# Stores of split weights issued from GpSimd's queue instead of SP's, in a hybrid decoder step

## The chip, the cores and the metric

The kernel runs on one core of a Trainium2 chip. The time is the device time in microseconds. The kernel before took 2448.59 us in the median of three runs (2443.82 to 2450.43). A profile is one further execution, in which every engine's instructions and every transfer were recorded.

## The reference

One layer of a decoder, for a prompt of 4096 rows and 8 single sample rows, all in float32, D_MODEL = 1024:

```python
u, zp, q, k, v, za, gp, ga = split_projection(rmsnorm(xp, g_norm[l]), w_in[l])
pooled = multiscale_pool(u, 0, seq)                       # trailing means over 2/4/8/16 rows
att = attn_prompt(q, k, v, rel_bias, attn_sinks[l])       # window of 128, sinks, T5 bias
pg = einsum(pooled, w_grp)                                # per channel group
br_pool = (pg * pool_scale * silu(z_pool)) @ w_br_pool
br_attn = (att * silu(z_attn)) @ w_br_attn
merged = sigmoid(g_pool) * br_pool + sigmoid(g_attn) * br_attn
y = rmsnorm(x + merged @ w_out, g_final)
```

The large pieces are the input projection (1024 columns in, 4352 out, by groups of 128 columns), the two branch projections and the output projection.

## The kernel before, in words

The rows are worked through in eight chunks of T = 512 (chunk 1 carries the 8 sample rows too). A product is made with three matmuls in a reduced float32 format: every operand is split into a high half and a low half (what the high half leaves over), and high x high, high x low and low x high are added up (`mm3`, L175 to L177). A weight tile `w` is [128, 2, 4, 128]: the two halves of four 128x128 blocks, 512 KB. `split_into` makes it from a raw tile `wr`: ScalarE copies the high half (L136), VectorE or GpSimd subtracts to get the low half (L137). In chunk 0 VectorE always subtracts; from chunk 1 on GpSimd does it for some.

The input projection takes two column groups and two row halves as a 2x2 block product with seven multiplications in place of eight (`Pair`). Three of its seven weights (11, 12, 22) are raw quarters. The other four (s1 to s4) are sums and differences of quarters. In chunk 0 they are made by VectorE in `combined` (L196, tiles `sr` and, in place, `wr`), split, multiplied, and also written to a DRAM tile `s...`, so that later chunks load the finished halves and neither add nor split. The 16 weight tiles of the output projection (`so`) and that of the group maps (`swg`) are treated in the same way. This is `kept(key, make)`: the first time a key is seen the tile is split and stored (the store is L169), afterwards it is loaded (L165). There are 68 + 16 + 1 = 85 stores, all in chunk 0.

Buffers set the pace. `w` tiles come from a ring of five; when `more_weights` has run, near the end of chunk 0, three of every eight tiles come from a second ring of three. A buffer of the ring can be filled again when TensorE has read it and, in chunk 0, the store has read it too. Raw tiles come from two rings of four (`wr`, and `wr0` that exists in chunk 0 alone), and pairs of 512 columns of x and intermediate results from a ring of five (`H`).

At the end of a chunk the output projection runs (L165 or L169 for its weights, L847 for the residual), and between its column groups the next chunk's x is loaded (`prep_xt`, L364), normalised and split into the seven combinations `xt`. The reload of the first stored weight for chunk 1 is the seam between chunks 0 and 1.

All DMAs before the change are issued by SP, one queue, in order: an issue that waits for a semaphore holds all that come behind it. A scheduler that places instructions by the operations' assumed costs fixes, when the program is built, each engine's order of instructions; nothing is reordered on the chip. GpSimd's own work in chunk 0 is the power that makes the inverse root (L297), copies of the carry of the pooling (L673, L695), of the last block's keys and values (L626, L627) and of the sample rows' x (L366).

Of the kernel before, what the change touches and what calls it, by code (L numbers as in the profile page):

```python
# [10 lines left out]
F32 = mybir.dt.float32  # L11
# [35 lines left out]
def split_kernel(ctx, tc, i, o):  # L47
    nc = tc.nc
# [86 lines left out]
    def split_into(w, raw, eng=None):  # L135
        nc.scalar.copy(w[:, 0], raw)  # L136
        (eng or nc.vector).tensor_tensor(out=w[:, 1], in0=raw, in1=w[:, 0].bitcast(F32), op=ALU.subtract)  # L137

    def wtile():
        if "p1" in place:  # L140
            place["n"] += 1
            if place["n"] % 8 >= 5:
                cnt[0] += 1
                return place["p1"].tile([P, 2, 4, P], F32R, tag="w2", name=f"w_{cnt[0]}", bufs=3)
        return st([P, 2, 4, P], "w", 5, F32R)
# [13 lines left out]
    cache = {}  # L159

    def kept(key, make):

        w = wtile()
        if key in cache:
            nc.sync.dma_start(out=w.bitcast(F32), in_=cache[key])  # L165
            return w
        split_into(w, make())
        cache[key] = dp.tile([P, 2, 4, P], F32, tag=f"s{key}", name=f"s{key}")
        nc.sync.dma_start(out=cache[key], in_=w.bitcast(F32))  # L169
        return w  # L170

    def mm3(ps, w, nk, rhs, start=True, stop=True, k0=0, **kw):
# [31 lines left out]
    class Pair:  # L204
# [26 lines left out]
        def w(self, q):  # L231
            if q in self.pre:
                return self.pre.pop(q)
            if q[0] == "s":
                return kept(f"{q}_{self.ia}", self.make[q] if self.c == 0 else None)
            if self.c == 0:
                w = wtile()
                split_into(w, self.plain[q])
                return w
            return wquarter(self.ia if q[0] == "1" else self.ib, int(q[1]) - 1, self.eng)  # L240
# [340 lines left out]
    for c in range(NCH):  # L581
# [41 lines left out]
        w = TP if smp else T  # L623
# [82 lines left out]
        def pool_y(g, hz):  # L706
            wg = kept("wg", raw_wg)
            for e in range(2):
                for a, b in segs(c):
                    ps = ps_mm(b - a)  # L710
                    mm(ps, lhsT=wg[:, 0, g + e, :], rhs=yph[:, g + e, a:b], start=True, stop=False)
                    mm(ps, lhsT=wg[:, 0, g + e, :], rhs=ypl[:, g + e, a:b], start=False, stop=False)
                    mm(ps, lhsT=wg[:, 1, g + e, :], rhs=yph[:, g + e, a:b], start=False, stop=True)
                    nc.vector.scalar_tensor_tensor(out=hz[:, e, a:b], in0=ps, scalar=psc[:, g + e:g + e + 1],
                                                   in1=hz[:, e, a:b], op0=ALU.mult, op1=ALU.mult)
            nc.scalar.copy(yph[:, g:g + 2, 0:w], hz[:, :, 0:w])
            lo(ypl[:, g:g + 2, 0:w], hz[:, :, 0:w], yph[:, g:g + 2, 0:w])
# [115 lines left out]
        for e in range(KT):  # L833
            if e % 4 == 0:
                oy[e // 4] = big([P, 4, TP], F32, f"oy{e // 4}")
            if e % 2 == 0:
                xt = pair_tile()[:, :, 0:T]
                nc.sync.dma_start(out=xt, in_=i["xt"][c, :, e:e + 2, :])
            wo = [kept(f"o{e}_{half}", lambda: wraw(W_O + e, half)) for half in range(2)]
            for a, b in segs(c):  # L840
                ps = ps_mm(b - a)
# [102 lines left out]
```

## Time and profile before

| | us |
|---|---|
| median of three runs | 2448.59 |
| lowest and highest | 2443.82, 2450.43 |
| the profiled execution, its time | 2446.67 |
| the profiled execution, its span | 2444.9 |
| TensorE busy | 2363.1 |
| VectorE busy | 1650.8 |
| ScalarE busy | 1146.0 |
| GpSimd busy | 310.0 |

The span goes from the first instruction to the last; the execution's own time has 1.8 us around it. Chunk 0 takes about 363 us of the span. In rows of the timeline and of groups stand the line, the engine, the operation, and out<-in by the program's names without buffer numbers; what stands in brackets is the idle time of the engine before the instruction and who ended it. SPq is SP's queue of DMA issues. A time "to landing" goes from a DMA's issue to the semaphore that tells that all of it has been written.

### The profile page before, as it was taken

The page shows a single profiled execution, that of the slowest core. Times are in us where ns is not written, and L with a number is a line of the kernel's source. Part 1 is how long each engine was busy: PE and PEld are TensorE (multiplying, and loading weights), DVE is VectorE, ACT ScalarE, POOL GpSimd, SP SyncE. Part 2 cuts the span into 40 slices and gives each one's busy share as a digit, 9 for nine tenths or more (in the row PEclk, how much of TensorE's full clock was granted, in tenths as well). Part 3 has the DMA queues.
Part 4 walks back from the last instruction along what each step waited for, and adds up shares of the span by engine and source line. Part 5 has one row for each costly group of instructions (what it writes and reads, how often), then busy time and mean ns, then how long its engine had stood idle before and what let it go on. Part 6 is the DMA issues. An engine that isn't in the chain of part 4 may idle for free.

```text
span 2444.9 us, 43970 instructions
## 1 busy us (share of the span) xinstructions
PE 2363.1 (97%) x16551; PEld 2198.0 (90%) x16551; DVE 1650.8 (68%) x3208; ACT 1146.0 (47%) x2324; POOL 310.0 (13%) x258
## 2 busy tenths in 40 slices
PE   7989999999999999999999999999999999999997
PEld 6878879999999988999889998899888998899986
DVE  6998776865668656686566855677556775668652
ACT  4667534563245633465234642456423563245531
POOL 0000001310024000330003300042001410013000
PEclk9989999999999999999999999999999999999998
DMA  6756688876686667767677666776667776687653
GB/s 203 255 194 245 226 282 322 227 244 219 223 279 239 237 231 242 272 232 245 212 256 266 236 229 233 246 267 237 228 233 260 248 239 231 233 279 246 215 196 141
DMA packets 231903, 583.60 MB, mean 239 GB/s; under 512 B 36315, under 2 KB 38652, under 8 KB 231692
## 3 DMA queue, kind: packets, MB, share of 16 engines
q1 hardware_dynamic: 231692, 580.80, 69.3%
q8 instruction: 131, 2.15, 0.3%
q14 instruction: 80, 0.66, 0.1%
HBM read 516.30 MB, written 64.40 MB: 238 GB/s over the span
## 4 chain that ended last, share of the span: by engine, by line
PE 68%; DVE 16%; DMA 7%; ACT 4%; issue 3%; SPq 0%; POOL 0%; DVEq 0%; ACTq 0%; POOLq 0%
PE hb L175 12%; PE hb L177 12%; PE hb L176 12%; PE mm L177 9%; PE mm L175 9%; PE mm L176 8%; DMA H<-in_xt 3%; DMA wr<-in_xq 2%; DVE oy L569 2%; DVE w L137 2%; PE tp L433 2%; PE pv L444 2%; DVE H L675 1%; DVE xt L180 1%; ACT LL L414 1%
## 5 line engine op out<-in xcount | busy, mean ns | idle before, releaser
L175 PE MATMUL hb<-xt,w 128*128 128x256 f32 x3316 | 945.3, 285 | 33.5 <-DVE U L268 13.3
L177 PE MATMUL hb<-xt,w 128*128 128x256 f32 x3316 | 941.4, 284 | 7.0 <-DVE w L137 7.0
L176 PE MATMUL hb<-xt,w 128*128 128x256 f32 x3316 | 938.2, 283 | 3.1 <-DVE xt L180 3.0
L175 PEld LDWEIGHTS hb<-xt,w 128*128 128x128 f32 x3316 | 633.2, 191 | 46.6 <-DVE H L272 15.1
L177 PEld LDWEIGHTS hb<-xt,w 128*128 128x128 f32 x3316 | 632.5, 191 | 10.1 <-DVE w L137 9.9
L176 PEld LDWEIGHTS hb<-xt,w 128*128 128x128 f32 x3316 | 632.8, 191 | 6.1 <-DVE xt L180 4.3
L136 ACT CAST w<-wr 128x512 fp32r<-128x512 f32 x570 | 349.5, 617 | 324.3 <-PE hb L177 202.2
L137 DVE TENSOR_TENSOR w<-wr,w 128x512 fp32r<-128x512 f32 x402 | 275.6, 689 | 141.1 <-ACT w L136 135.8
L137 POOL TENSOR_TENSOR w<-wr,w 128x512 fp32r<-128x512 f32 x168 | 251.6, 1501 | 500.5 <-ACT w L136 409.7
L175 PE MATMUL mm<-mh,w 128*128 128x512 f32 (+1 forms) x576 | 213.8, 371 | 2.4 <-ACT w L136 2.3
L177 PE MATMUL mm<-mh,w 128*128 128x512 f32 (+1 forms) x576 | 213.6, 371 | 0.8 <-DVE w L137 0.8
L176 PE MATMUL mm<-ml,w 128*128 128x512 f32 (+1 forms) x576 | 213.0, 370 | 0.3 <-DVE ml L809 0.3
L297 POOL TENSOR_TENSOR rs<-rs,nhalf 128x4 f32<-128x4 f32 (+1 forms) x18 | 17.9, 999 | 1338.9 <-DVE rs L295 1338.8
L801 DVE SCALAR_TENSOR_TENSOR H<-H,mm 128x512 f32<-128x512 f32 (+1 forms) x144 | 90.3, 628 | 111.9 <-PE mm L177 111.6
L414 ACT ACTIVATE LL<-LL,nm 128x257 f32<-128x257 f32 (+1 forms) x256 | 126.5, 496 | 65.9 <-DVE nm L411 65.8
L175 PE MATMUL mm<-xt,w 128*128 128x260 f32 x476 | 135.9, 286 | 2.0 <-DMA w<-ss 1.3
L177 PE MATMUL mm<-xt,w 128*128 128x260 f32 x476 | 134.8, 284 | 1.1 <-POOL w L137 0.6
L176 PE MATMUL mm<-xt,w 128*128 128x260 f32 x476 | 134.6, 283 | 0.0
L281 DVE TENSOR_TENSOR H<-hb,U 128x512 f32<-128x512 f32 x119 | 81.9, 688 | 73.3 <-PE hb L177 71.0
L175 PEld LDWEIGHTS mm<-mh,w 128*128 128x128 f32 x576 | 108.5, 188 | 22.4 <-ACT w L136 2.8
L177 PEld LDWEIGHTS mm<-mh,w 128*128 128x128 f32 x576 | 108.6, 189 | 22.0 <-DVE w L137 1.9
L847 DVE TENSOR_TENSOR oy<-mm,H 128x512 f32<-128x512 f32 (+1 forms) x72 | 45.1, 630 | 122.9 <-PE mm L177 93.1
(193 smaller groups left out, 4113.8 us busy)
## 6 DMA issues: line engine op xcount, KB each, us to landing
w<-ss SPq DMA_DIRECT2D x476, 512.0 KB, 4.4
wr<-in_wall SPq DMA_DIRECT2D x569, 256.0 KB, 3.4
w<-so SPq DMA_DIRECT2D x112, 512.0 KB, 4.0
ss<-w SPq DMA_DIRECT2D x68, 512.0 KB, 3.2
H<-in_xt SPq DMA_DIRECT2D x32, 512.0 KB, 5.6
wr<-in_xq SPq DMA_DIRECT2D x56, 256.0 KB, 3.0
H<-in_xt SPq DMA_DIRECT2D x56, 256.0 KB, 5.7
out_y<-oy SPq DMA_DIRECT2D x28, 512.0 KB, 4.6
```

The costliest lines, as they stand in the source:

```text
L136: nc.scalar.copy(w[:, 0], raw)
L137: (eng or nc.vector).tensor_tensor(out=w[:, 1], in0=raw, in1=w[:, 0].bitcast(F32), op=ALU.subtract)
L175: mm(ps, lhsT=w[:, 0, k0 + k, :], rhs=rh, start=start and k == 0, stop=False, **kw)
L176: mm(ps, lhsT=w[:, 0, k0 + k, :], rhs=rl, start=False, stop=False, **kw)
L177: mm(ps, lhsT=w[:, 1, k0 + k, :], rhs=rh, start=False, stop=stop and k == nk - 1, **kw)
L281: nc.vector.tensor_tensor(out=self.mid, in0=self.R, in1=u2.unsqueeze(1).to_broadcast([P, 2, n]), op=ALU.add)
L414: nc.scalar.activation(out=L[:, j, k0:2 * P + 1], in_=L[:, j, k0:2 * P + 1], func=AF.Exp, bias=nm[:, j:j + 1], accum_out=den[:, j:j + 1])
L433: nc.tensor.transpose(tp[:, j, :], L[:, j, kb * P:(kb + 1) * P], ident)
L444: mm(pv, lhsT=vs[:, b + kb, g, :], rhs=pt[:, kb, m].rearrange("p j q -> p (j q)"), start=n == 0 and m == 0, stop=n == len(kbs) - 1 and m == 1)
L569: nc.vector.scalar_tensor_tensor(out=y, in0=y, scalar=gf[:, e:e + 1], in1=rsp[:, 0:n], op0=ALU.mult, op1=ALU.mult)
L801: nc.vector.scalar_tensor_tensor(out=t[:, a:b], in0=t[:, a:b], scalar=1.0, in1=ps, op0=ALU.add, op1=ALU.mult)
L847: nc.vector.tensor_tensor(out=y[:, e % 4, a:f], in0=ps[:, 0:f - a], in1=xt[:, e % 2, a:f], op=ALU.add)
```

## The change

The store of a split weight is issued from GpSimd instead of SP. Nothing else in the text differs:

```diff
@@ -166,7 +166,7 @@
             return w
         split_into(w, make())
         cache[key] = dp.tile([P, 2, 4, P], F32, tag=f"s{key}", name=f"s{key}")
-        nc.sync.dma_start(out=cache[key], in_=w.bitcast(F32))
+        nc.gpsimd.dma_start(out=cache[key], in_=w.bitcast(F32))
         return w
```

The scheduler places some instructions anew in chunk 0 and in the first pairs of chunk 1, and leaves all that follows as it was. Three places show it. The first is SP's queue in the output projection of chunk 0 (`so` are its stored weights, `wr` its raw ones, `H<-in_xt` the next chunk's x):

```order
-L169 DMA so_0_3502<-w_3497 128x1024
+L149 DMA wr_3601<-in_wall 128x512
 L364 DMA H_3537<-in_xt 128x512 x2
-L149 DMA wr_3601<-in_wall 128x512
-L169 DMA so_1_3509<-w_3504 128x1024
 L149 DMA wr_3608<-in_wall 128x512
-L169 DMA so_0_3560<-w_3555 128x1024
-L169 DMA so_1_3567<-w_3562 128x1024
-L169 DMA so_0_3605<-w_3600 128x1024
-L169 DMA so_1_3612<-w_3607 128x1024
 L149 DMA wr_3659<-in_wall 128x512
```

The six stores are gone from between the raw loads, which now follow one another. The second place is SP's queue at the end of chunk 0, where the last raw loads, the sample rows' caches (`kv`) and the first reload for chunk 1 (`w_3932<-ss_12_176`) stood:

```order
+L838 DMA H_3598<-in_xt 128x2x512
+L364 DMA H_3640<-in_xt 128x512 x2
 L149 DMA wr_3875<-in_wall 128x512
-L590 DMA kv_3915<-in_ck 128x8x127
-L169 DMA so_0_3872<-w_3867 128x1024
-L169 DMA so_1_3879<-w_3874 128x1024
-L591 DMA kv_3915<-in_cv 128x8x127
-L165 DMA w_3932<-ss_12_176 128x1024
 L149 DMA wr_3946<-in_wall 128x512
```

The last raw load of the output weights now stands right behind the second pair of x (before, it stood behind the fourth), the stores are gone, and the caches and the reload have moved to behind the third pair of x. The third place is GpSimd's own queue in the middle of chunk 0, around the second pooling group:

```order
 L673 COPY H_1424<-carry 128x2x16
+L169 DMA ss_2_1567<-w_1563 128x1024
 L695 COPY carry<-H_1424 128x32
+L169 DMA ss_6_1630<-w_1626 128x1024
+L169 DMA ss_6_1664<-w_1661 128x1024
+L169 DMA ss_6_1682<-w_1678 128x1024
+L169 DMA ss_6_1769<-w_1765 128x1024
```

The stores stand in the order in which the weights are split, with the carry's copies among them.

## The prediction

> **What bounds the kernel now.** I read the page first, then busy time by stretch, then the waits of SP's queue, and last the timelines at the places where the stores stand.
>
> ```profile
> span 2444.9 us, 43970 instructions
> PE 2363.1 (97%) x16551; PEld 2198.0 (90%) x16551; DVE 1650.8 (68%) x3208; ACT 1146.0 (47%) x2324; POOL 310.0 (13%) x258
> ```
>
> TensorE is busy 97% of the span, so little can be won anywhere. But the moved stores exist only in chunk 0, the first of eight, and the shares of that stretch are others (columns of the rows below: PE, PEld, DVE, ACT, POOL busy, granted clock, DMA share, GB/s):
>
> ```profile
> 40.00:220.00 180.00, 162.94 (x1176) 150.92 (x1176) 167.83 (x343) 116.59 (x252) 8.64 (x7) 0.95 0.62 221
> 220.00:340.00 120.00, 119.73 (x710) 105.02 (x709) 93.63 (x161) 61.70 (x115) 3.30 (x8) 1.00 0.72 255
> 340.00:420.00 80.00, 74.06 (x513) 67.46 (x512) 53.56 (x100) 31.78 (x61) 7.81 (x10) 0.98 0.91 327
> ```
>
> From 40 to 220 us VectorE is the bound (167.83 of 180 us): it makes the combinations and the low halves of every weight. From 220 to 340 TensorE is (119.73 of 120), and nothing that the change does there can help. From 340, at the seam to chunk 1, TensorE stands idle 5.94 us while the DMA engines are 91% busy. Only the first and the last stretch can move.
>
> What does SP, which issues every DMA, wait for? Its queue's waits over the first 360 us (us in total, times, longest), and the stores' own view:
>
> ```profile
> SPq L169 <- DVE w L137: 131.7, 72, 11.7
> SPq L191 <- DVE sr L196: 34.2, 9, 7.5
> L169 SPq DMA_DIRECT2D ss<-w x68: 319/326/514, 25.9 to 283.6; - x68
> DMA to landing us min/median/max: 2.6/3.2/6.2
>   ACT w L136: 1.1, 3
> ```
>
> SP stands 131.7 us in front of stores whose weight is not split yet, and every load behind them stands too. Yet someone must miss those loads for it to cost. So the question is where a load comes late.
>
> **The change, part by part.**
>
> *(a) SP no longer stops at stores.* 85 issues of 0.326 us leave its queue. Between 40 and 220 us I give this nothing: the loads of raw weights stand a whole pair ahead of their use, their own wait there is for free raw buffers (L191, 34.2 us), and VectorE works on 93% of the stretch. If that cover were gone, 12.2 us, all of VectorE's idle time there, is the most there is. At the seam it is different. SP's issues there, start and length:
>
> ```profile
> 307.15 0.42 SPq L149 DMA_DIRECT2D wr<-in_wall  x1
> 317.28 2.77 SPq L169 DMA_DIRECT2D so<-w  x4
> 351.07 0.33 SPq L169 DMA_DIRECT2D so<-w  x1
> 351.44 1.27 SPq L149 DMA_DIRECT2D wr<-in_wall  x2
> 357.01 2.14 SPq L169 DMA_DIRECT2D so<-w  x2
> 359.85 0.80 SPq L165 DMA_DIRECT2D w<-ss  x1
> ```
>
> and the DMA engines and TensorE meanwhile:
>
> ```profile
> 300.00:320.00 20.00, 20.00 (x89) 16.07 (x88) 16.70 (x29) 7.97 (x14) 1.44 (x4) 1.00 0.45 159
> 320.00:340.00 20.00, 20.00 (x88) 16.18 (x87) 12.64 (x22) 7.95 (x12) 0.32 (x2) 1.00 0.97 338
> 340.00:360.00 20.00, 16.93 (x65) 12.57 (x64) 16.13 (x28) 6.81 (x10) 0.31 (x2) 0.91 0.81 286
> ```
>
> SP is stuck from 307.6 to 317.3 before a store, with the DMA engines at 45%; then they run at 97%, and the loads of the last output weights go out at 351.4, behind one more store; the first reload for chunk 1 goes at 359.85, behind two. The one who waits:
>
> ```profile
> 355.34 0.62 ACT L136 CAST w<-wr 128x512 fp32r<-128x512 f32 x1 [1.82 <-DMA wr<-in_wall]
> 351.10 0.50 PE L177 MATMUL mm<-mh,w 128*128 128x512 f32 x1 [0.75 <-DVE w L137]
> 356.01 0.62 PE L175 MATMUL mm<-mh,w 128*128 128x512 f32 x1 [2.32 <-ACT w L136]
> 359.72 0.39 PE L177 MATMUL mm<-mh,w 128*128 128x512 f32 x1
> 359.95 0.40 PE L175 MATMUL mm<-mh,w 128*128 128x512 f32 x1
> 364.90 0.39 PE L175 MATMUL mm<-xt,w 128*128 128x260 f32 x1 [1.31 <-DMA w<-ss]
> 367.57 0.39 PE L177 MATMUL mm<-xt,w 128*128 128x260 f32 x1 [0.54 <-DVE w L137]
> ```
>
> The raw weight is late, ScalarE's copy is late, TensorE waits 2.32 us, and after that gap its matmuls start (359.72 - 356.01)/8 = 0.46 us apart against 0.23 (359.72 to 359.95): eight steps, 1.85 us more (the 0.91 of granted clock). The reload costs 1.31 us. In the changed order the last raw loads stand before transfers of the input that they stood behind, the reload before the cache loads, and no store is between. I take these three away: 2.32 + 1.85 + 1.31 = 5.5 us. The other two gaps (0.75 and 0.54) come through VectorE's order and stay in the sum; with them the gain would be 6.8, which is the upper end. The lower end is zero, if the waits come back (rival B).
>
> *(b) A store lands later, and its buffer with it.* In chunk 0 five buffers w go round. A buffer is free again when TensorE has read it and the store has landed. One place, all four rows of it: the store at 75.23, ScalarE's copy into the same buffer five tiles on (the first of the two that start at 78.20), and VectorE's part of that tile (the first of the pair at 79.55); and a place where the profile itself names the store:
>
> ```profile
> 75.23 0.33 SPq L169 DMA_DIRECT2D ss<-w  x1
> 78.20 1.14 ACT L136 CAST w<-wr 128x512 fp32r<-128x512 f32 x2
> 79.55 1.29 DVE L137 TENSOR_TENSOR w<-wr,w 128x512 fp32r<-128x512 f32 x2
> 66.58 0.62 ACT L136 CAST w<-wr 128x512 fp32r<-128x512 f32 x1 [0.22 <-DMA ss<-w]
> ```
>
> With the median of 3.2 us the store lands at 78.4; ScalarE needs 0.62 us, and VectorE comes to it at 79.55: a reserve of 79.55 - 0.62 - 78.43 = 0.5 us, by which this store may be later at no cost. The same difference for each of the 49 stores between 40 and 220 us gives small reserves at six places: 0.5, 0.5, 1.2, 1.25, 1.5 and 2.0; the next is 2.5. The last of the six in time, for a check (store, VectorE's part: 172.59 - 0.62 - 170.72 = 1.25):
>
> ```profile
> 167.52 0.33 SPq L169 DMA_DIRECT2D ss<-w  x1
> 172.59 0.69 DVE L137 TENSOR_TENSOR w<-wr,w 128x512 fp32r<-128x512 f32 x1
> ```
>
> So if GpSimd's store lands d us later than SP's, VectorE loses what d exceeds each reserve by: 1.0 us at d = 1, 5.1 at d = 2, 11.9 at d = 3, 34 at d = 5. After 220 us VectorE has 22% to spare, and I charge nothing.
>
> What is d? No DMA from GpSimd is in the trace. Below: -0.6, the fastest SP store against the median (2.6 and 3.2). Above: GpSimd's copy of the carry, which does almost nothing,
>
> ```profile
> L695 POOL COPY carry<-H x16: 209/1297/5227, 113.8 to 2236.3; 128x32 f32<-128x32 f32 x16
> 150.22 5.23 POOL L695 COPY carry<-H 128x32 f32<-128x32 f32 x1 [30.33 <-DVE H L281]
> L297 POOL TENSOR_TENSOR rs<-rs,nhalf x18: 538/1006/1347, 19.3 to 2433.0; 128x4 f32<-128x4 f32 x16, 8x1 f32<-8x1 f32 x2
> ```
>
> takes 0.21 us when left alone and 5.23 us at 150.22 in chunk 0, where VectorE runs without a break: 5.0 us more. The instruction nearest in kind, one with hardly any data whose time is its own fixed work, is the power of L297 at 1.0 us, against 0.33 for an SP issue; with a store queued behind another now and then I take d = 1, which costs 1.0 us. The Trainium skill ("DMA: Bandwidth & Descriptors", Anatomy of one DMA) gives for GpSimd's path some 2.0 us plus the bytes over 436 GB/s: an estimate of 3.2 us for 512 KB, which is SP's measured 3.2; with it d would be nought and the sum 1.0 us lower. No run here shows it.
>
> *(c) GpSimd's own work stands behind stores.* It is busy 8.64 of 180 us, so 49 stores of about 1 us fit. Two things cost nothing under a cover. The copy of 5.23 us now stands before the store that SP issues at 150.72; that one goes about 5 us later, and VectorE comes to the next tile in its buffer at 166.81, 12 us after it used to land. And the four pairs of small copies into H for chunk 1 stand behind a store or two, while x itself travels into the same tiles for 5.7 us; without that cover they would cost 4 x 1 us.
>
> ```profile
> 150.72 0.33 SPq L169 DMA_DIRECT2D ss<-w  x1
> 166.81 0.68 DVE L137 TENSOR_TENSOR w<-sr,w 128x512 fp32r<-128x512 f32 x1
> H<-in_xt SPq DMA_DIRECT2D x56, 256.0 KB, 5.7
> ```
>
> *(d) GpSimd's issues hold VectorE.* Its subtraction in the pooling, L686, takes 680 ns, but 1787 at worst, in later chunks where GpSimd splits weights beside it:
>
> ```profile
> L686 DVE SCALAR_TENSOR_TENSOR H<-H,H x32: 677/680/1787, 117.3 to 2243.1; 128x512 f32<-128x512 f32 x32
> ```
>
> Chunk 0 has four of these: 0 to 4 x 1.1 = 4.4 us. GpSimd would be busy about a quarter of the time and the overlap is partial; I take 0.5.
>
> **Sum.** Against the profiled execution's own 2446.67 us (span 2444.9 and 1.8 around it): -5.5 + 1.0 + 0.5 = -4.0, so 2442.7. That execution lies 1.9 below the median of the runs, 2448.59; on the median's scale the forecast is 2444.6 us, 0.16% faster. A measurement of this kernel can tell 0.3% from no change, 7.3 us: faster begins below 2441.2, slower above 2455.9.
>
> **Rivals.**
>
> *B. Nothing is won: the DMA engines, not SP, hold the seam.* The bytes are the same, and they move at 97%, 81% and 91% of the engines' time. Then the loads wait in the engines as they did in the queue, and (b) and (d) remain: 2446.67 + 1.5 + 1.9 = 2450.1. For it: 338 GB/s at 320 to 340 us. Against: the 45% just before. The Trainium skill says on the same page (Issuing engines are not separate DMA queues) that issuing from several engines saves only issue time; by that rule (a) is nought here. The trace bears out that issue time is not it (85 x 0.326 = 28 us on an idle SP), but the rule does not speak of an in-order queue that stands before a wait.
>
> *C. Slower: GpSimd cannot issue while VectorE runs without a break.* Place: 40 to 220 us, where VectorE works on 93%. Price: with d = 4, between my value and the copy's 5.0, the reserves (those of 2.5, 2.8, 3.0 and over included) give 21 us: 2446.67 - 5.5 + 21 + 0.5 + 1.9 = 2464.6; with d = 5, 2477. It decides from d = 3, where 11.9 us eat the gain. For it: the copy's 5.23. Against: that copy is a rare case, one like it (L673) took 0.67 us at 72.74 in the same stretch, and it moves data through GpSimd itself, which an issue does not.
>
> ```profile
> 72.74 0.67 POOL L673 COPY H<-carry 128x32 f32<-128x32 f32 x1
> ```
>
> The Trainium skill names this ("SBUF — State Buffer", the "DVE blocks DMA" trap): GpSimd cannot write descriptors while VectorE runs in a mode that takes the shared port. By that page two-input operations, which fill this stretch, stop only operations of GpSimd that read SBUF, so the rule as it stands speaks for a small d; the row of 5.23 agrees with the part on reads.
>
> *D. A clear gain.* All five gaps go (6.8), d is nought or below (three waits, 1.1 us, go too) and GpSimd holds nobody: 2446.67 - 7.9 + 1.9 = 2440.7.
>
> That the change would not do what it says is excluded: the list of instructions has all 85 stores on GpSimd's queue, and SP's order differs from before only to the end of chunk 0 and the first pairs of chunk 1.
>
> **How the numbers follow.** Forecast 0.43, B 0.22, C 0.20, D 0.15. The forecast's own range is 2441 to 2450. To leave out no more than 2 in 10 it reaches to D below (2439) and to C at d of nearly 4 above (2462). Faster: D and a little of the forecast, 0.18; slower: C and a little of B, 0.22; the same 0.60.
>
> **What would show it.** (a) right: no DMA or ScalarE wait of TensorE over 1 us between 345 and 370 us, and the DMA share from 300 to 320 above 0.6; wrong: the share still 0.97 later and waits of the same sum. (b) right: stores landing about 4 us after VectorE's part, and ScalarE's waits for ss<-w between 40 and 220 at about 2 us in all; wrong: stores landing after 6 us or more, and the time at which VectorE begins the output weights later by 10 us. (d): L686 in chunk 0 above 0.7 us. The forecast falls if TensorE's idle time from 340 to 420 us (5.94 now) does not fall by at least 3 us, or if a stretch after 500 us takes another time than before.

## The result, and the profile after

The changed kernel takes 2464.24 us (median) against 2446.97 us of the kernel before on the same chip: a ratio of 1.0074, with a 95% interval of 1.0054 to 1.0094. It is slower, by 17.3 us. The forecast was 2444.6 us with a range to 2462; it was wrong. The profiled execution took 2463.62 us; the head of its page, and its stretches in the columns of the prediction (PE, PEld, DVE, ACT, POOL busy, granted clock, DMA share, GB/s):

```profile
span 2461.7 us, 44029 instructions
PE 2361.6 (96%) x16551; PEld 2197.6 (89%) x16551; DVE 1652.8 (67%) x3208; ACT 1144.9 (47%) x2324; POOL 361.7 (15%) x343
```

```profile
40.00:220.00 180.00, 159.47 (x1157) 148.06 (x1157) 165.54 (x339) 113.17 (x247) 34.15 (x54) 0.96 0.61 218
220.00:340.00 120.00, 112.48 (x675) 98.83 (x675) 88.55 (x150) 59.25 (x113) 18.26 (x36) 0.99 0.67 239
340.00:420.00 80.00, 69.73 (x433) 62.85 (x433) 49.34 (x85) 32.43 (x59) 7.70 (x12) 0.91 0.83 296
300.00:320.00 20.00, 20.00 (x89) 16.07 (x89) 14.03 (x22) 8.93 (x17) 1.92 (x5) 1.00 0.63 215
```

TensorE's busy time is that of before (2361.6 against 2363.1); what is new is idle time, and 85 more instructions on GpSimd, the stores. From 220 to 340 us, where TensorE had been busy 119.73 us of 120, it now stands idle 7.5; from 340 to 420 it stands idle 10.27 us where it stood 5.94, and at a clock of 0.91 for 0.98.

To see where time goes, one compares when the same piece of work starts in two profiles. The table does this for the main kernels of this study: start of the same VectorE split (L137), up to 297 us, and then of the same later ScalarE or VectorE instruction (L620, L847), minus its start in the profile of before (the n-th instruction of a line against the n-th, so that single places are shifted where the order differs). All are us; each row is one execution.

| start before | 75 | 105 | 215 | 261 | 297 | 413 | 1049 | 2390 |
|---|---|---|---|---|---|---|---|---|
| changed kernel | 0.0 | 1.7 | 2.6 | 8.2 | 9.2 | 22.1 | 18.5 | 17.9 |
| path_only | -0.6 | 2.1 | 2.3 | 4.3 | 4.2 | 5.8 | 6.7 | 4.7 |
| order_only | 0.4 | 0.2 | -0.5 | 4.3 | 5.3 | 18.1 | 18.1 | 21.2 |
| ss_only | -0.2 | 1.2 | 2.3 | 7.6 | 8.2 | 8.4 | 7.1 | 9.5 |
| so_only | -0.6 | -0.6 | -1.6 | -0.9 | -1.0 | 10.1 | 12.3 | 11.2 |
| sp_order | 0.1 | 2.7 | 3.3 | 7.8 | 6.8 | 8.9 | 5.3 | 6.7 |
| rest_order | -0.8 | 1.7 | 1.8 | 4.8 | 4.6 | 7.8 | 8.3 | 12.4 |
| x_first | 0.5 | 2.2 | 3.3 | 8.7 | 9.7 | 21.0 | 18.4 | 12.2 |
| wr5_old_sp | 0.3 | 0.3 | -0.2 | 0.5 | 0.4 | 1.2 | -1.7 | -13.0 |
| wr5_old_pool | -0.6 | 2.1 | 2.3 | 2.8 | 3.8 | 5.4 | 0.3 | -7.9 |

Its first row: 2.6 us are lost by 215 us, 6.6 more from there to 297, and 12.9 at the seam, from 297 to 413; after that some 4 come back. In this execution chunks 1 to 7 cost nothing more.

What SP waits for up to 360 us, in the changed kernel (us in total, times, longest):

```profile
SPq L191 <- DVE w L137: 91.4, 34, 9.8
SPq L149 <- DVE w L137: 59.5, 27, 10.1
```

SP stood 131.7 us before stores (L169). That row is gone, and SP now stands before loads of raw weights (L191, L149) until VectorE's split has freed one of their buffers: the same releaser, one queue entry further on. At the seam, SP's issues and TensorE's waits:

```profile
315.90 23.17 SPq L149 DMA_DIRECT2D wr<-in_wall  x10
340.35 3.27 SPq L364 DMA_DIRECT2D H<-in_xt  x2
343.72 12.29 SPq L149 DMA_DIRECT2D wr<-in_wall  x4
356.06 1.83 SPq L838 DMA_DIRECT2D H<-in_xt  x1
358.06 2.40 SPq L364 DMA_DIRECT2D H<-in_xt  x2
371.85 0.82 SPq L364 DMA_DIRECT2D H<-in_xt  x2
```

```profile
372.37 0.39 PE L175 MATMUL mm<-xt,w 128*128 128x260 f32 x1 [1.02 <-ACT xt L384]
382.11 0.59 PE L175 MATMUL mm<-xt,w 128*128 128x260 f32 x1 [7.67 <-ACT xt L384]
428.74 0.58 PE L175 MATMUL mm<-xt,w 128*128 128x260 f32 x1 [3.28 <-DVE H L271]
```

Ten raw loads take 23.17 us of SP's queue, and the second pair of chunk 1's x (L364) behind them goes out at 340.35 us, 16.7 us later than before (323.62). Four more, three of them for chunk 1, take 12.29 us because there is no buffer for them, and the third and fourth pair stand behind. The fourth goes out at 371.85 us, 24.9 us later than before (346.96), and TensorE waits 7.67 us for what is made of it. No such wait was in the profile of before.

The seam is more than this one wait. The next table takes it apart by TensorE's own matmuls, the n-th of the changed kernel against the n-th of before (start minus start, us; three kernels of the experiments below stand beside it):

| start before | 312 | 342 | 365 | 373 | 405 | 415 |
|---|---|---|---|---|---|---|
| changed kernel | 9.1 | 12.4 | 5.5 | 17.7 | 17.6 | 22.3 |
| order_only | 5.3 | 11.6 | 4.7 | 14.8 | 14.8 | 18.0 |
| so_only | -1.0 | 3.5 | -3.4 | 5.7 | 5.6 | 10.2 |
| path_only | 4.2 | 4.3 | 3.1 | 5.8 | 5.8 | 5.8 |

The changed kernel loses 3.3 us by 342, wins 6.9 by 365, loses 12.2 by 373, where x is late, and 4.7 more by 415. The gain is the one that was forecast: the last two raw loads of the output weights go out 12.7 and 8.2 us earlier than before, and from 345 to 370 us TensorE waits for nothing. The last loss begins with the wait of 3.28 us for VectorE at 428.74; what makes VectorE late there was not followed.

The stores themselves (GpSimd's issues of the combined weights; below, who waited, and the time to landing):

```profile
L169 POOL DMA_DIRECT2D ss<-w x68: 531/531/772, 26.2 to 293.1; - x68
  ACT w L136: 8.4, 6
DMA to landing us min/median/max: 2.9/4.5/8.3
```

```profile
77.17 0.69 DVE L137 TENSOR_TENSOR w<-sr,w 128x512 fp32r<-128x512 f32 x1
78.27 0.53 POOL L169 DMA_DIRECT2D ss<-w  x1 [2.10 <-DVE w L137]
```

A store takes GpSimd 0.53 us, begins 0.41 us after the end of the split that it waits for (78.27 - 77.86; the median is 0.40, and on SP 0.03), and lands 4.5 us after its issue, against 3.2 on SP. The 4.5 is the median of all 85 stores; the 3.2 is that of 11, since the trace of before tells the landing of no more of SP's stores. ScalarE's waits for landed stores rise from 1.1 us (3 times) to 8.4 (6).

### The profile page after: what moved, and what is told of

It is laid out like the page before. It is cut to its first block, busy times and chain, and to the rows that moved or that the text cites. A ratio compares the mean times of both kernels' runs of the same rounds, so it can differ in the third digit from the quotient of the medians.

```text
span 2461.7 us, 44029 instructions
## 1 busy us (share of the span) xinstructions
PE 2361.6 (96%) x16551; PEld 2197.6 (89%) x16551; DVE 1652.8 (67%) x3208; ACT 1144.9 (47%) x2324; POOL 361.7 (15%) x343
## 4 chain that ended last, share of the span: by engine, by line
PE 67%; DVE 14%; DMA 8%; issue 7%; ACT 3%; POOL 1%; SPq 0%; DVEq 0%; ACTq 0%; POOLq 0%
PE hb L175 11%; PE hb L176 11%; PE hb L177 11%; PE mm L175 9%; PE mm L177 9%; PE mm L176 9%; DMA H<-in_xt 3%; DMA wr<-in_xq 2%; DVE oy L569 2%; PE pv L444 2%; PE tp L433 2%; DVE w L137 1%; DVE H L675 1%; DVE xt L180 1%; DVE H L376 1%
## 5 line engine op out<-in xcount | busy, mean ns | idle before, releaser
L177 PE MATMUL hb<-xt,w 128*128 128x256 f32 x3316 | 939.0, 283 | 7.9 <-DVE w L137 7.8
L177 PEld LDWEIGHTS hb<-xt,w 128*128 128x128 f32 x3316 | 630.5, 190 | 11.0 <-DVE w L137 10.8
L136 ACT CAST w<-wr 128x512 fp32r<-128x512 f32 x570 | 350.0, 617 | 342.4 <-PE hb L177 196.2
L137 DVE TENSOR_TENSOR w<-wr,w 128x512 fp32r<-128x512 f32 x402 | 275.5, 687 | 150.7 <-ACT w L136 147.8
L137 POOL TENSOR_TENSOR w<-wr,w 128x512 fp32r<-128x512 f32 x168 | 253.9, 1515 | 499.0 <-ACT w L136 398.6
L177 PE MATMUL mm<-mh,w 128*128 128x512 f32 (+1 forms) x576 | 212.8, 369 | 0.0
L175 PE MATMUL mm<-xt,w 128*128 128x260 f32 x476 | 137.9, 290 | 12.2 <-ACT xt L384 8.7
L176 PE MATMUL mm<-xt,w 128*128 128x260 f32 x476 | 137.1, 288 | 1.6 <-DVE xt L180 1.6
L177 PE MATMUL mm<-xt,w 128*128 128x260 f32 x476 | 136.7, 288 | 0.0
L176 PEld LDWEIGHTS mm<-ml,w 128*128 128x128 f32 x576 | 108.2, 188 | 21.5 <-DVE ml L809 1.5
L177 PEld LDWEIGHTS mm<-mh,w 128*128 128x128 f32 x576 | 108.2, 188 | 20.1
```

Source lines behind the costliest of these rows:

```text
L175: mm(ps, lhsT=w[:, 0, k0 + k, :], rhs=rh, start=start and k == 0, stop=False, **kw)
L176: mm(ps, lhsT=w[:, 0, k0 + k, :], rhs=rl, start=False, stop=False, **kw)
L177: mm(ps, lhsT=w[:, 1, k0 + k, :], rhs=rh, start=False, stop=stop and k == nk - 1, **kw)
```

## The experiments

### Path or order: four kernels

Moving the stores changed two things: the way that a store goes, and the order that the scheduler makes of everything else when SP has no stores. To part them, the program is built twice in one file. The first build gives the order; the second ties each instruction to the one before it on its engine, the stores excepted:

```diff
-        nc.sync.dma_start(out=cache[key], in_=w.bitcast(F32))
+        moved.add(store(nc, key).dma_start(out=cache[key], in_=w.bitcast(F32)).ins.name)
...
+            for n in order:
+                x = seen.get(n)
+                if x is None or n in moved:
+                    continue
+                if x.engine in last:
+                    tc.add_manual_dep(x, last[x.engine], mybir.DependencyInfo(
+                        mybir.DependencyClass.NoSync, mybir.DependencyReason.DATA))
+                last[x.engine] = n
...
+    _, order = _build(arrays, lambda nc, key: nc.sync)
+    nc, _ = _build(arrays, lambda nc, key: nc.gpsimd, order)
```

The last two lines are those of path_only (`order` holds the names of the instructions as the first build placed them); order_only exchanges the two engines. ss_only and so_only are built once, without ties: `store` is `nc.sync if key[0] == "o" else nc.gpsimd`, and the reverse.

> All 85 stores on GpSimd's queue, but every other instruction of every engine stands in the order that it has in the kernel before. Before is 2446.97 us, the changed kernel 2464.24 (+17.3, of which its trace shows +2.6 by 220 us, some +7 from 220 to 300, +14 from 300 to 345, and about 6 given back later). Theory O (the new order does it: raw weights are loaded ahead of chunk 1's input, which comes late): this kernel has the old order and keeps only the later landing of the stores, about 1.7 us each. It loses 2.6 us before 220, at most some us from 220 to 300, and may win up to 5.5 at the seam: 2446 to 2452 us; H_530_3849's transfer for chunk 1 issued within 5 us of 347. Theory Q (GpSimd's path itself does it: a later and slower issue, and its own copies standing behind stores): 2460 to 2466 us, whatever the order.

> All 85 stores back on SP's queue, but every other instruction of every engine stands in the order that it has in the changed kernel. Theory O: the stretch before 220 us costs nothing (the stores land as before), the seam costs what it costs in the changed kernel, +14 with about 6 given back, and SP stops at stores besides: 2455 to 2464 us. Theory Q: 2444 to 2450 us, since no store goes by GpSimd.

> Only the 69 stores of combined weights (and the pooling weight) go by GpSimd; the 16 of the output weights stay on SP. The order of SP's loads at the seam is then that of before. Theory O: +2.6 before 220 us, up to 5 more before 300, nothing at the seam: 2449 to 2454 us, and TensorE idle from 340 to 420 us near the 5.94 of before. Theory Q: the same or a little more, 2450 to 2456.

> Only the 16 stores of the output weights go by GpSimd; the other 69 stay on SP. The order of SP's loads at the seam is then that of the changed kernel. Theory O: nothing before 300 us, +14 at the seam with some given back: 2455 to 2462 us. Theory Q: 16 of 85 stores, and few copies behind them: +1 to +6, 2448 to 2453 us.

| kernel | stores | order | median us | ratio (95%) |
|---|---|---|---|---|
| before | SP | old | 2448.01 | 1 |
| path_only | GpSimd | old | 2452.10 | 1.0023 (1.0012 to 1.0034) |
| order_only | SP | new | 2472.29 | 1.0100 (1.0084 to 1.0116) |
| changed kernel (its own comparison) | GpSimd | new | 2464.24 | 1.0074 (1.0054 to 1.0094) |
| ss_only | split | scheduler's | 2458.19 | 1.0048 (1.0031 to 1.0064) |
| so_only | split | scheduler's | 2458.32 | 1.0050 (1.0037 to 1.0063) |

Theory O holds, and more strongly than it was put: the order alone costs 24 us (1.00%), the path alone 0.23%. In the new order GpSimd's queue seems to help (1.0074 against 1.0100), but these are two comparisons whose intervals overlap. order_only came out 8 us above its expected 2455 to 2464. The seam is not the reason: at 413 us its profile is 18.1 us late and the changed kernel's 22.1; why its median is higher stays open. Its TensorE waits at the seam as the changed kernel's does, though no store goes by GpSimd:

```profile
379.06 0.58 PE L175 MATMUL mm<-xt,w 128*128 128x260 f32 x1 [7.96 <-ACT xt L384]
```

It also wins the same 6.9 us from 342 to 365 (11.6 to 4.7 in the table of the seam), though its stores are on SP. So gain and loss at the seam both belong to the order. so_only, where only the 16 output weights are moved, shows the same pattern (its raw loads hold SP for 13.61 us between two pairs of x) and loses all of its 11 us at the seam; ss_only keeps SP's old order at the seam and loses nothing there (8.2 at 297 us, 8.4 at 413):

```profile
332.74 13.61 SPq L149 DMA_DIRECT2D wr<-in_wall  x4
346.40 0.42 SPq L838 DMA_DIRECT2D H<-in_xt  x1
359.93 0.81 SPq L364 DMA_DIRECT2D H<-in_xt  x2
```

ss_only missed its 2449 to 2454 by 4 us: 5.3 us go between 215 and 261, where the order differs too, against 2.0 in path_only.

path_only (0.1 us above its range) is the test of what step (a) named as the cause: the old order, and no store on SP. SP's waits for VectorE from 300 to 360 us, of before and then of path_only:

```profile
SPq L169 <- DVE w L137: 31.3, 15, 9.7
SPq L149 <- DVE w L137: 2.8, 1, 2.8
SPq L364 <- DVE xt L180: 2.4, 1, 2.4
```

```profile
SPq L149 <- DVE w L137: 22.2, 10, 10.2
SPq L364 <- DVE xt L180: 9.3, 2, 5.7
SPq L364 <- DVE H L803: 2.6, 1, 2.6
SPq L838 <- DVE acc L865: 2.1, 1, 2.1
```

36.5 us have become 36.2 (a row of 0.3 is left out): VectorE holds SP as long as it did, now before raw loads and x instead of before stores. What TensorE waits for has changed all the same. First before, then path_only, at the same weight, the last but one of the output:

```profile
353.72 0.69 DVE L847 TENSOR_TENSOR oy<-mm,H 128x512 f32<-128x512 f32 x1 [0.87 <-PE mm L177]
356.30 0.69 DVE L137 TENSOR_TENSOR w<-wr,w 128x512 fp32r<-128x512 f32 x1
357.04 0.80 PE L177 MATMUL mm<-mh,w 128*128 128x512 f32 x1
```

```profile
357.67 0.62 ACT L136 CAST w<-wr 128x512 fp32r<-128x512 f32 x1
357.98 0.69 DVE L847 TENSOR_TENSOR oy<-mm,H 128x512 f32<-128x512 f32 x1 [0.87 <-PE mm L177]
358.34 0.51 PE L175 MATMUL mm<-mh,w 128*128 128x512 f32 x1 [0.40 <-ACT w L136]
360.55 0.69 DVE L137 TENSOR_TENSOR w<-wr,w 128x512 fp32r<-128x512 f32 x1
361.29 0.50 PE L177 MATMUL mm<-mh,w 128*128 128x512 f32 x1 [2.21 <-DVE w L137]
```

The raw load is no longer late: ScalarE copies the weight without a wait for it (1.82 us before), and TensorE waits 0.40 us for the copy and not 2.32. But two matmuls on, it needs the low half, and VectorE makes that in its own order, the old one, behind the residual of the output (L847) and the normalising of x. From L847 to TensorE's L177 it takes 3.31 us (361.29 - 357.98); before, with the raw load late, it took 3.32 (357.04 - 353.72). So in the old order the late load cost TensorE nothing of its own: VectorE's split held it to the same moment. At the reload it is alike. Its wait of 1.31 us is gone, and a wait of 1.01 us for ScalarE's copy of the next weight has come, and one of 1.04 for VectorE's split of it (0.54 before). The seam gains nothing; it loses 1.6 us (4.2 to 5.8 in both tables). What path_only loses before it, it loses in two places, at 80 us and from 222 to 261. In both ScalarE waits for a landed store; in the second this shows once, 1.62 us at 230.88. The first:

```profile
80.58 0.62 ACT L136 CAST w<-wr 128x512 fp32r<-128x512 f32 x1 [2.35 <-DMA ss<-w]
81.23 0.69 DVE L137 TENSOR_TENSOR w<-wr,w 128x512 fp32r<-128x512 f32 x1 [1.58 <-ACT w L136]
```

### Whose order?

sp_order ties SP alone to the old order, rest_order all engines but SP (one comparison with `mybir.EngineType.SP` in the loop above). x_first leaves the changed kernel to the scheduler with one rule more:

```diff
-        nc.sync.dma_start(out=raw, in_=i["wall"][idx][:, 4 * half:4 * half + 4, :])
+        with tc.issue_after(state["x"]) if "x" in state else ExitStack():
+            nc.sync.dma_start(out=raw, in_=i["wall"][idx][:, 4 * half:4 * half + 4, :])
...
-                nc.sync.dma_start(out=xt[:, e, 0:T], in_=i["xt"][c, :, kk + 4 * e, :])
+                state["x"] = nc.sync.dma_start(out=xt[:, e, 0:T], in_=i["xt"][c, :, kk + 4 * e, :]).ins
```

> All 85 stores on GpSimd; of the old order only SP's is kept, the other four engines are ordered anew by the scheduler. Theory S (what costs is SP's order: loads of raw weights, those of chunk 1 among them, stand before chunk 1's input and wait for one of four raw buffers): 2450 to 2455 us, like the kernel with the whole old order (2452.1), and TensorE's gap of 7.67 us at 374 gone. Theory V (what costs is the order of VectorE, ScalarE and TensorE, which make the split of weights early and the input late): 2458 to 2465 us.

> The other half of the same cut: all 85 stores on GpSimd, VectorE, ScalarE, TensorE and GpSimd's own work in the old order, SP ordered anew. Theory S: 2457 to 2468 us, if the scheduler again puts raw loads before the input; theory V: 2450 to 2455 us.

> The changed kernel with one rule more: a load of raw weights that is written behind a load of chunk input also stands behind it on SP; nothing else is ordered by hand. At the seam the last input pair then stands before the raw weights wr_533, wr_535 and all of chunk 1's. Theory S: about 10 us of the changed kernel's 17 come back (the 7.67 us gap and the half-speed matmuls behind it), 2450 to 2456 us; the losses by the later landing and from 220 to 300 us stay. Theory V: 2460 to 2466 us.

sp_order takes 2455.15 us (1.0029, 1.0020 to 1.0038; the upper end of S's range), rest_order 2457.6 (1.0039, 1.0024 to 1.0054). With SP's order held the seam is nearly undone: the profile loses 2.1 us there (6.8 to 8.9) and not 12.9, and the gap of 7.67 us is not in it. But neither kernel parts theory S from theory V, because what was left free came out nearly old as well. By names, without buffer numbers, 23 of SP's 1400 other issues stand in another place than of old in rest_order, and 61 in the changed kernel. In sp_order 15 of TensorE's matmuls between 363 and 500 us do, and 100 in the changed kernel; of VectorE's instructions there 5, and 43. The crossed kernels, SP's new order with the others' old one and the reverse, were not run. So it stays open whose order costs how much.

x_first (2458.66 us, 1.0047, 1.0029 to 1.0065) missed: theory S, in the form "raw loads ahead of x are the harm", expected the seam's loss back. By the ratios it is 6.6 us better than the changed kernel (0.27%), with intervals that overlap, but the first table shows that little of this is at the seam (9.7 at 297 us, 21.0 at 413: 11.3 lost for 12.9); it comes after 1049 us, where the rule changes SP's order too. At the seam other waits have come. SP's issues, and the waits of TensorE and ScalarE:

```profile
329.15 3.80 SPq L150 DMA_DIRECT2D wr<-in_wall  x4
339.05 0.38 SPq L838 DMA_DIRECT2D H<-in_xt  x1
345.67 0.81 SPq L364 DMA_DIRECT2D H<-in_xt  x2
346.57 3.56 SPq L150 DMA_DIRECT2D wr<-in_wall  x4
```

```profile
345.08 0.50 PE L175 MATMUL mm<-mh,w 128*128 128x512 f32 x1 [2.68 <-ACT w L136]
361.46 0.79 PE L175 MATMUL mm<-mh,w 128*128 128x512 f32 x1 [2.54 <-ACT w L136]
379.86 0.79 PE L177 MATMUL mm<-mh,w 128*128 128x512 f32 x1 [3.81 <-DVE w L137]
```

```profile
343.37 0.62 ACT L383 CAST xt<-H 128x520 fp32r<-128x520 f32 x1 [2.76 <-DVE H L369]
343.90 1.13 ACT L136 CAST w<-wr 128x512 fp32r<-128x512 f32 x2
```

SP issues no raw load from 332.95 to 346.57, because tiles of x (for the output's sum, L838, and for chunk 1, L364) wait at the head of its queue for their buffers. Yet from 325 to 385 us ScalarE never waits for a raw load. What makes TensorE wait is the order of ScalarE and VectorE: the copy of a weight (L136 at 343.90) stands behind the work on x (L383), which waits 2.76 us for VectorE. So the theory has to be put differently. Raw loads and x share SP's in-order queue, each waits for a buffer that VectorE frees, and the kernels with the new order show that raw loads ahead of x hold it up. The splits of weights and the work on x share the queues of ScalarE and VectorE in the same way, and there path_only and x_first lose. Which of these orders is worth how much no kernel here separates.

### The landing, made later

In path_only each weight is stored twice, first to a place that nobody reads:

```diff
-            moved.add(store(nc, key).dma_start(out=cache[key], in_=w.bitcast(F32)).ins.name)
+        for to in ([dp.tile([P, 2, 4, P], F32, tag=f"t{key}", name=f"t{key}")] if store(nc, key) is nc.gpsimd else []) + [cache[key]]:
+            moved.add(store(nc, key).dma_start(out=to, in_=w.bitcast(F32)).ins.name)
```

> The stores on GpSimd in the old order (2452.1 us, +2.2 of it by 220 us and +2.0 from 222 to 265), and each weight is stored twice, first to a place that nobody reads: the store that counts is issued at least 0.53 us later, its buffer comes free 0.5 to 2 us later still, and 45 MB more are written. If the later landing is what costs in that kernel: +4 to +8 by 220 us, 2455 to 2462 us in all. If it is something else (GpSimd's work beside VectorE's): +2 to +3 by 220 us, 2452 to 2454.

It takes 2484.87 us (1.0155, 1.0139 to 1.0172), far over the 2455 to 2462 expected. By 215 us it is 13.9 us late, path_only 2.3; ScalarE waits 22.8 us (13 times) for stores. From 40 to 220 us a store lands 6.2 us after its issue (median; 4.5 in path_only), and it is issued 0.53 us later, behind its copy. The stretch:

```profile
40.00:220.00 180.00, 153.37 (x1087) 142.44 (x1087) 154.84 (x314) 104.74 (x227) 55.69 (x97) 0.93 0.90 336
```

So some 2.2 us of landing cost 11.6 us: the reserves are soon used up, as the prediction's list had it (3.6 us lost at 1.7, 21 at 4), only somewhat less steeply. The test is not clean: the DMA engines are busy 0.90 of that stretch for 0.63, so loads may be late as well.

### The raw buffer

If SP waits for raw buffers, a fifth should show. The first three kernels differ from those above by `"wr", 5)` for `"wr", 4)` at its four places. wr5 is path_only with it; wr5_sp is the same with SP's stores; wr5_before is the kernel before with that number alone, wr5_free the changed kernel with it.

> The stores on GpSimd in the old order (2452.1 us) and five raw buffers wr for four. In that kernel SP stands 10.24 us at 321.58 before the raw load wr_504, where before it stood 9.71 us before a store. If raw buffers are what holds SP there (and so eat the gain that I had put at 5.5 us): the wait moves one load on, wr_504 goes out some 10 us earlier, and the raw loads behind it one buffer earlier; yet the last two, wr_533 and wr_535, stand behind the input pair H_530, which waits for VectorE, so the gap of 2.21 us at 359 stays, and the time is 2450 to 2453 us. If they were held by raw buffers alone, the gap goes and the time is 2446 to 2449.

> The kernel before, in its own order, stores on SP, with five raw buffers wr for four (the kernel with stores on GpSimd, this order and five was 2444.7 us against 2448.07 of before, and 2452.1 with four). Theory J (two waits stand in one queue one behind the other, the stores and the raw buffers; to take one away gives nothing): SP still stands 9.7 us before a store at 307 to 317, the fifth buffer can't be filled earlier, and the time is 2446 to 2450 us. Theory R (the raw buffer alone is the gain, and the stores only cost their later landing): some 4 us better than with the stores on GpSimd, 2439 to 2443 us.

> The kernel before with five raw buffers and the scheduler free to order anew (stores on SP). Theory J: 2446 to 2452 us; theory R: 2439 to 2443. A third outcome, above 2455, would say that the scheduler's new order costs here too, with no store moved.

> The changed kernel with five raw buffers and the scheduler free to order anew. If the changed kernel's loss is the order that the scheduler makes when it thinks SP free (raw loads as far ahead as buffers allow, the input behind them): 2455 to 2466 us, as with four, since the loads only run further ahead. If the loss is the shortage of raw buffers itself: 2445 to 2452 us.

| kernel | stores | order | median us | ratio (95%) |
|---|---|---|---|---|
| wr5 | GpSimd | made for five, stores on SP | 2444.70 | 0.9985 (0.9973 to 0.9998) |
| wr5_sp | SP | the same | 2442.64 | 0.9984 (0.9975 to 0.9994) |
| wr5_before | SP | the same | 2441.72 | 0.9974 (0.9964 to 0.9984) |
| wr5_free | GpSimd | made for five, stores on GpSimd | 2465.03 | 1.0070 (1.0056 to 1.0083) |

Two things were not as the expectations say, and wr5 came out below both of its ranges (2446 to 2449 and 2450 to 2453). "The old order" of wr5 and wr5_sp is the one that the first build made with five buffers, and on SP that is not the order of before; and wr5_sp and wr5_before are one and the same program, measured twice (2442.64 and 2441.72). Theory J fell: the buffer gains with the stores on SP as with the stores on GpSimd. And wr5_free says once more that the order is the loss: with five buffers it costs 0.70%, as with four. To part buffer and order, the last two kernels take the order from a build with four buffers and then make the ring five:

```diff
     _, order = _build(arrays, lambda nc, key: nc.sync)
+    raws[0] = 5
     nc, _ = _build(arrays, lambda nc, key: nc.gpsimd, order)
```

(wr5_old_sp has `nc.sync` there and ties the stores too, so that every instruction stands as before.)

> The kernel before, every instruction of every engine in its own order, stores on SP; only the ring of raw buffers has five places for four. (In the earlier kernels with five the scheduler had made the order for five, which differs from the old one on SP; here the buffer is the one difference.) If the buffer by itself is the gain: 2440 to 2444 us, and the gaps of 0.75 and 2.32 us at 350 to 356 gone. If the gain lay in the order that the scheduler makes for five: 2446 to 2450 us, and the gaps stay, since SP issues the last two raw loads behind the fourth input pair and a store.

> The same with all 85 stores on GpSimd: the old order, five raw buffers. My step (a) in its purest form, no store and no lack of a raw buffer in front of the raw loads, though the input pairs still are. If step (a) only lacked the buffer: 5.5 us better than the same kernel with four (2452.1), 2444 to 2448 us. If the input pairs hold the raw loads at the seam: 2450 to 2453 us.

wr5_old_sp takes 2433.55 us, 0.9937 (0.9923 to 0.9950); wr5_old_pool 2439.32, 0.9964 (0.9951 to 0.9976). The first is the fastest kernel of this study, 14.4 us under before. Both are below their ranges, and the gain is not where either expectation had it. The seam is unchanged: both profiles are no faster at 413 us than without the buffer (1.2 late, and 5.4 against 5.8), and the gap is still there in wr5_old_pool:

```profile
361.00 0.50 PE L177 MATMUL mm<-mh,w 128*128 128x512 f32 x1 [2.22 <-DVE w L137]
```

This gap is VectorE's once more: from L847 (at 357.69) to TensorE's L177 it takes the same 3.31 us. The gain lies in chunks 2 to 7, some 2.5 us in each (1.8 late at 727 us, 13.0 early at 2390), where SP had waited for raw buffers all along. TensorE's own waits there, from 720 to 2400 us, fall from 28.2 to 19.0 us; what makes up the rest of the gain is not shown. SP's waits from 720 to 2400 us, of before and of wr5_old_sp:

```profile
SPq L149 <- DVE w L137: 261.1, 144, 6.5
SPq L149 <- POOL w L137: 216.6, 97, 5.5
```

```profile
SPq L149 <- DVE w L137: 84.0, 69, 3.3
SPq L149 <- POOL w L137: 32.7, 40, 1.3
```

And with the order and the ring the same, stores on GpSimd cost 5.8 us (2439.32 - 2433.55), as with four buffers (0.23%).

## Why the prediction was wrong

**(a), -5.5 us at the seam: the gain came, and the step failed in what it put at nothing.** As the prediction put it: "In the changed order the last raw loads stand before transfers of the input that they stood behind, the reload before the cache loads, and no store is between. I take these three away". The waits that it priced did go. From 345 to 370 us TensorE waits for nothing, and from 342 to 365 it wins 6.9 us, beside the 6.8 that was the upper end. Both signs that were given for (a) came true, the second with a DMA share of 0.63 from 300 to 320 us. But that raw loads now stand ahead of the input was counted as a gain alone. What the input then waits for was not asked, and its delay stood in the sum at nothing: the raw loads wait up to 10.1 us for a buffer, the fourth pair of x goes out 24.9 us later, and right behind the 6.9 won TensorE loses 12.2. With 3.3 lost ahead of it and 4.7 behind, the seam costs 13.2 us by TensorE's matmuls where the sum had -5.5.

The cause that (a) named was wrong as well. It is not that SP no longer stops at stores: order_only has the stores on SP and wins the same 6.9 us, and path_only has none there and wins 1.2, to lose 2.7 right behind. In the old order splits by VectorE and ScalarE stood directly behind the waits that were taken away, and the rows of before could have told: VectorE's split of the weight that came late ended at 356.99, and TensorE's L177 began at 357.04. The new order moves VectorE's work as well (from 297 to 363 us 56 of its instructions stand in another place, by line).

**From 220 to 297 us the sum had nothing, and 6.6 us went.** The prediction said of this stretch that TensorE is its bound, "and nothing that the change does there can help". It did not ask whether something could hurt. order_only loses 5.8 us there and path_only 1.9, so most of it is the order; which wait it is was not followed.

**(b), later landing: mechanism right, size too small.** d was taken as 1; it measured (4.5 - 3.2) + 0.4 = 1.7 us, where the 3.2 rests on 11 of SP's 85 stores. The place was right: the first reserve of the list, at 79.55 us, is where ScalarE waits 2.35 us. By the list's own reserves 1.7 gives 3.6 us before 220; path_only lost 2.3. "After 220 us VectorE has 22% to spare, and I charge nothing" was wrong by 2.0 us: the spare share is an average, and at 230.88 us a single split had no reserve for its store. The Trainium skill ("DMA: Bandwidth & Descriptors", Anatomy of one DMA) would have had 3.2 us to landing for 512 KB, an estimate by its formula; the measured median is 4.5.

**(c), nothing for GpSimd's own work: right in the old order** (path_only loses nothing around the carry's copy: 2.1 to 2.3 us late from 105 to 215), and nearly so in the changed kernel, where SP waits 1.1 us once for GpSimd's small copies into H, which stand behind stores of weights whose split is late.

**(d), GpSimd holding VectorE, +0.5: nothing.** L686 in chunk 0 took 677 to 680 ns before, and beside the stores

```profile
L686 DVE SCALAR_TENSOR_TENSOR H<-H,H x4: 675/681/686, 119.0 to 159.4; 128x512 f32<-128x512 f32 x4
```

**The rivals.** C named the measured time within 0.4 us (2464.6 for 2464.24), by chance: its place, 40 to 220 us, gave 2.6 us and not 21, and d stayed below the 3 from which it was to decide. The part of the Trainium skill's rule weighed there ("SBUF — State Buffer", the "DVE blocks DMA" trap: two-input operations stop only GpSimd's reads) agrees: 0.41 us from split to issue in the densest stretch. B's outcome, nothing won at the seam, is what path_only shows (2452.1 for its 2450.1), but not by B's mechanism: from 340 to 420 us none of TensorE's waits in path_only is for a DMA. For the rule that stood beside B, that issuing from several engines saves only issue time (the Trainium skill, "DMA: Bandwidth & Descriptors", Issuing engines are not separate DMA queues), the trace of path_only agrees in the result, for a reason that the rule does not give: VectorE's and ScalarE's splits stood right behind the waits that went.

**The sentence that hid the loss.** "SP's order differs from before only to the end of chunk 0 and the first pairs of chunk 1." This excluded a rival; it should have been one. What the change cost beyond its 0.23% by path lies in this "only". The prediction's own test, that idle time from 340 to 420 us must fall by 3 us, went the other way, from 5.94 to 10.27.

## What to carry to other kernels

When a wait is taken away, ask what stands right behind it, in the queue and in the engine that waited: in path_only TensorE got its weight's high half in time and then waited for the low half, and nothing was won. When an order changes, price what moves back as well as what moves forward: here 12.2 us were lost right behind the 6.9 that were won. Where a scheduler sets the order, a moved instruction moves others; hold the old order and run both halves before putting a loss down to the instruction. And a queue that waits on the way, hundreds of us in all, for one kind of buffer is a reason to try one buffer more before any new queue: that was worth 14 us here, more than the best case of the change (7.9).

## What the runs showed that was not expected

A store of 512 KB from GpSimd holds GpSimd for 0.53 us, starts 0.41 us after the split that releases it and lands 4.5 us after its start (2.9 to 8.3), 1.7 us later in all than the 11 stores from SP whose landing is known; with two such stores at a time the median was 6.2. VectorE's work beside them kept its duration to within 1%. And one order of the same instructions against another was worth 24 us (1.00%) with not one instruction changed; of the 21.0 us by which its profiled execution is longer than that of before, 18.6 were lost in the 200 us from 215 to 413.
